# Weight halves of a float32 layer: split once and kept in DRAM, in place of split in every block

## The chip, the cores and the metric

The kernel runs on one core of a Trainium2 chip. The metric is the time of one execution on the device, in microseconds (us). TensorE (PE) multiplies; its weight loader is a row of its own in the profile (PEld). VectorE (DVE), ScalarE (ACT) and GpSimd (POOL) do the rest of the arithmetic, and SyncE (SP) and ScalarE issue the DMAs. Each engine runs its stream of instructions in order.

## The reference, cut to what matters

One layer of a hybrid model runs over 2048 prompt tokens with 16 meta tokens ahead of them, and over 8 sample sequences of 8 tokens. All is float32.

```python
h = rms_norm(x, norm_w)
proj = jnp.einsum('btd,de->bte', h, w_in)
...
new_dn_s, o_dn = run_chunks(gated_delta_chunk, dn_s, (q, k, v, g, beta), is_prompt)
...
(new_c, new_n, new_m), h_ml = run_chunks(mlstm_chunk, (ml_c, ml_n, ml_m), (q, k, v, ig, lf), is_prompt)
...
y5, new_re, new_im = s5_mixer(s5_re, s5_im, s5_u, ...)
y5 = y5 * jax.nn.sigmoid(y5 @ f32(s5_w_glu) + f32(s5_b_glu))
...
mixed = (gates[:, :, 0] * (o_dn @ w_branch_dn)
         + gates[:, :, 1] * (o_ml @ w_branch_ml)
         + gates[:, :, 2] * (o_s5 @ w_branch_s5))
x = x + mixed @ w_out
```

The products with `w_in`, `s5_w_glu`, the three `w_branch` and `w_out` are the dense products of this text. The recurrences (gated delta rule, mLSTM, S5) stand between them.

## The kernel before, in words

The tokens are columns and lie in six blocks (`BLOCKS`, L30): block 0 has the samples, the meta tokens and two tiles of 128 prompt tokens (336 columns), blocks 1 to 4 three tiles (384 columns), block 5 two (256 columns). Each block runs the whole layer: normalisation, the token rows (`rows`, "rX" and its fellows in the trace), the S5 scan, the projections, the recurrences, the mixing and the output. The order of the steps in a block is written out by hand (`PLAN0`, `PLAN`); within that a scheduler orders the instructions of each engine by priority and by its own simulated time.

A dense product (`product`, L229) multiplies in three passes, so that float32 is kept: weight and activation are each split into two exact halves, and for every 128 rows k of the weight there are three matmuls, high by high, high by low, low by high. All dense matmuls have the line 196, a helper, and write "pd". A weight tile is four such k, [128, 4, 128] float32, 256 KB, so one weight tile serves 12 matmuls. The line of the helper for two-operand arithmetic is 185.

The halves of a weight tile come from `weights` (L217): SP loads the tile "w" from DRAM (L222), ScalarE casts it to the high half "wh" (L223), and VectorE or GpSimd subtracts to get the low half "wl" (L226, L185 in the trace). In the first block every fourth subtract goes to GpSimd, later every second. This happens for every tile in every block; the weights are the same. There are four buffers for "w", three for "wh" and three for "wl" (`WB`), and the three instructions have a raised priority (`WPRIO`), so they are placed ahead of other work.

SP also issues the other loads and the transfers through DRAM: the S5 input and output ("us", "ys", stored from "s5u" and "s5y"), the S5 matrices ("s5w", "s5t") and the small blocks of the delta rule's inverse ("scrp", "scru"). ScalarE's queue issues "ox" and the output.

Of the kernel before, what the change touches and what calls it, by code (L numbers as in the profile page):

```python
# [9 lines left out]
F32 = mybir.dt.float32  # L10
F32R = mybir.dt.float32r
# [16 lines left out]
# Prompt tiles of 128 tokens per block; the first block also has the tile of samples and meta tokens.  # L28
# [8 lines left out]
WB = (4, 3, 3)  # L37
UNITS = 12
# Order of the steps of the first block and of the others: projections of q, k, v (d, m), recurrences, outputs.
# [5 lines left out]
# Buffers of temporaries: floats of a partition, and how many.  # L45
# [17 lines left out]
# Column blocks of the input projection, in the order in which the host lays them out.  # L63
CB_S5U, CB_DN, CB_ML, CB_MLO, CB_MLZ, CB_S5Z, CB_DNZ, CB_GATE = 0, 4, 16, 28, 32, 36, 40, 44

# Columns of the array of vectors.
V_NW, V_TAP, V_BG, V_DNN, V_MLN, V_S5D, V_BGLU, V_FN, V_RB, V_AL, V_LDT, V_LR, V_LI, NV = (
    0, 8, 56, 80, 81, 82, 86, 90, 98, 99, 100, 116, 132, 148)
# Columns of the array of constants.
# [34 lines left out]
class Kernel:  # L104
    def __init__(self, ctx, tc, I, O):
        self.ctx, self.tc, self.nc, self.I, self.O = ctx, tc, tc.nc, I, O
        nc = tc.nc
        self.V, self.A, self.G, self.E = nc.vector, nc.scalar, nc.gpsimd, nc.tensor
        pool = lambda n, b, **k: ctx.enter_context(tc.tile_pool(name=n, bufs=b, **k))
        self.cp = pool("const", 1)  # L110
        self.xp = pool("xn", 1)
        self.gp = pool("units", UNITS)
        self.wp = pool("weights", 2)
        self.tp = pool("temps", 2)
        self.sp = pool("small", 2)
        self.pd = pool("pdense", BANKS["pd"], space=PSUM)
        self.pr = pool("prec", 5, space=PSUM)
        self.uid = 0
        self.wn, self.rb = 0, None

# [20 lines left out]
    def temp(self, shape, tag, dt=F32):  # L141
        """A tile of a set of buffers that several steps share."""
        group = GROUP[tag]
        size, bufs = POOL[group]
        n = int(np.prod(shape[1:]))
        assert n <= size, (tag, shape)
        t = self.tp.tile([P, size], dt, name=self.name(tag), tag=group, bufs=bufs)
        v = t[:shape[0], 0:n]
        if len(shape) == 3:
            v = v.rearrange("p (a b) -> p a b", a=shape[1])  # L150
        elif len(shape) == 4:
            v = v.rearrange("p (a b c) -> p a b c", a=shape[1], b=shape[2])
        elif len(shape) == 5:
            v = v.rearrange("p (a b c d) -> p a b c d", a=shape[1], b=shape[2], c=shape[3])
        return v

    def pair(self, w, name):
        """Two tiles of the four heads, the second of width w, in one unit."""
        u = self.unit([P, 4 * P + 4 * w], name=name)
        return u[:, 0:4 * P].rearrange("p (h n) -> p h n", h=4), u[:, 4 * P:].rearrange("p (h n) -> p h n", h=4)  # L160
# [41 lines left out]
    def rsqrt(self, out, x, shape, also_sqrt=None):  # L202
        """out = 1/sqrt(x) on a small tile of positive floats: a first guess from their bits, three Newton steps."""
# [13 lines left out]
    def weights(self, src, k0):  # L217
        w = self.wp.tile([P, 4, P], F32, name=self.name("w"), tag="w", bufs=WB[0])
        h = self.wp.tile([P, 4, P], F32R, name=self.name("wh"), tag="wh", bufs=WB[1])
        l = self.wp.tile([P, 4, P], F32R, name=self.name("wl"), tag="wl", bufs=WB[2])  # L220
        with self.tc.high_priority(offset=WPRIO if self.wn > 1 else 5500):
            self.nc.sync.dma_start(w, src[:, k0:k0 + 4])  # L222
            self.A.copy(h, w)  # L223
            self.wn += 1
            pool = WPOOL if self.b else WPOOL0
            self.tt(self.G if pool and self.wn % pool == 0 else self.V, l, w, h, OP.subtract)  # L226
        return h, l
# [12 lines left out]
    def proj(self, cb):  # L240
        return self.product(self.I["wi"][cb], 8, lambda k: self.xh[k // 4][:, k % 4, :],
                            lambda k: self.xl[k // 4][:, k % 4, :], self.T)

# [1 line left out]
    def setup(self):  # L245
# [18 lines left out]
        # the row groups' bias with its sign, and the rows' factor of softplus  # L264
# [19 lines left out]
    def block(self, b):  # L284
# [20 lines left out]
        # (first column, sequences, their length): chunks over which decays are summed  # L305
        self.segs = ([(0, 8, 8), (NS, 1, NM)] if self.first else []) + [(self.p0, BLOCKS[b], P)]

    def norm(self):
        """xn^T = x^T * norm_w * rstd, as two exact halves."""
# [12 lines left out]
        if self.first:  # L322
            # x^T * norm_w in halves, for the products that need not wait for rstd
# [37 lines left out]
    def rstd_row(self, acc):  # L361
        """1/rms of every token, in every partition of a row, from squares summed over k."""
# [16 lines left out]
    def bc(self, src, c0, ns, L, p0, p1, at):  # L379
        """[p, ns, L]: of each sequence its column `at`, repeated."""  # L380
# [6 lines left out]
    def rows(self):  # L387
        T, V, A, b = self.T, self.V, self.A, self.b
        ps = self.product(self.I["ws"], 8, lambda k: self.xh[k // 4][:, k % 4, :],
# [9 lines left out]
        # softplus(u) = max(u, 0) + 2 artanh(e / (2 + e)), e = exp(-|u|)  # L399
# [17 lines left out]
        # cumulative sums by chunk: G in rows 0.., b in rows 32..  # L417
# [10 lines left out]
        # running maximum; M[:, 1 + t] is m after token t, M[:, 0] the block's first m  # L428
# [26 lines left out]
        # rows that go to all partitions: G; b - m; b + m(chunk start) - m  # L455
# [12 lines left out]
        # rows that become columns: G, G_last - G | ig - b, its state weight, -m | beta  # L468
# [11 lines left out]
    def columns(self):  # L480
        """The rows as columns of the tiles, their exponentials, and the rows as operands of products that spread them."""
# [22 lines left out]
        # halves of the rows, masked by head, as operands of the products that spread them  # L504
# [12 lines left out]
    def spread(self, i, g):  # L517
        """Rows of group g for tile i, by head, in every partition."""
# [6 lines left out]
    def dn_proj(self, n):  # L525
        """Projection, convolution and SiLU of column block n of q, k, v."""
# [35 lines left out]
    def dn_pre(self):  # L562
# [22 lines left out]
        for i, (o, n) in enumerate(self.tiles):  # L585
# [11 lines left out]
            # the squares of k are on the diagonal  # L597
# [32 lines left out]
    def dn_inv(self):  # L630
        """Inverses of the 32 x 32 blocks of I + P on the diagonal, one block per partition."""
# [22 lines left out]
    def dn_merge(self, i):  # L654
        """The whole inverse of tile i from its diagonal blocks."""
# [42 lines left out]
    def tok(self, src, o, n):  # L698
        """Token-major columns of the four heads."""
# [8 lines left out]
    def dn_tile(self, i):  # L708
# [9 lines left out]
        if n < P:  # L718
            # kept until the samples' states are updated
# [53 lines left out]
    def dn_samples_in(self, x):  # L773
        """For the samples: x -= e^G k s; returns q s, with its decay, in the upper partitions."""
# [3 lines left out]
        for h in range(4):  # L778
            # for every sequence 64 columns of k and 64 of q with those of the others zero
# [16 lines left out]
    def samples_update(self, h, states, out, left, right, decay):  # L796
        """Each sequence's state: state * decay + left^T right over its own tokens."""
# [17 lines left out]
    def factors(self, ss, other):  # L815
        """1/sqrt(ss/128 + eps*other) by token and head."""
# [8 lines left out]
    def finish(self, raw, f, gate, scale, name):  # L825
        """Branch output, feature-major and in two halves: (raw * f)^T * scale * gate(h)."""
# [16 lines left out]
    def silu2(self, cb):  # L843
        """z * (1 + tanh(z/2)) of a projected column block."""
# [92 lines left out]
    def by_sequence(self, x, tag):  # L937
        """Of the samples' columns of a head, [128, 8, 8]: for every sequence 64 columns with those of the others zero."""
# [6 lines left out]
    def ml_samples_in(self):  # L945
        """The states of the samples, and q * n."""
# [45 lines left out]
    def s5_powers(self):  # L992
        """The transition, its powers and phase, and the inputs' factor."""
# [30 lines left out]
        # powers of the transition; pw[k] = a^k  # L1024
# [10 lines left out]
        # phase of a^4  # L1035
# [4 lines left out]
        # (a - 1) / lambda  # L1040
# [13 lines left out]
    def s5_setup(self):  # L1054
        """The group matrices of four steps at a time, into DRAM: input to output, to state, from state; phases."""
# [31 lines left out]
        # powers 3, 2, 1, 0 for the inputs; 0 .. 4 for the outputs  # L1087
# [4 lines left out]
        def spread(out, pk, r, K, tag):  # L1092
            """Blocks k of out, on the diagonal of the pair: power k times r, (re + im, im - re) of r or the like."""
# [52 lines left out]
    def feat(self, d, f):  # L1146
        """Features of column block f, by step and chunk."""
        return d[:, P * f:P * f + P, 0:self.s5n].rearrange("j f c -> f j c")

    def pairs(self, d, f, j):  # L1150
        """Step j of the four pairs of groups of column block f."""
        return d[j, P * f:P * f + P, 0:self.s5n].rearrange("(a q) c -> q a c", q=32)

    def s5_scan(self, f):
# [57 lines left out]
        if self.first:  # L1212
            # samples: two chunks each from their own state
# [28 lines left out]
    def s5_finish(self):  # L1242
# [20 lines left out]
        for f in range(4):  # L1263
            ps = self.product(self.I["wg"][f], 4, lambda k: yh[:, k], lambda k: yl[:, k], T)
# [14 lines left out]
    def mix(self, j, first, last):  # L1279
        """acc += (1 + tanh(gate / 2)) * (product of branch j); the last branch leaves the sum in halves."""  # L1280
# [7 lines left out]
        for d in range(8):  # L1288
# [5 lines left out]
            pb = self.product(self.I["wb"][c], 4, lambda k: h[:, k], lambda k: l[:, k], T)  # L1294
# [9 lines left out]
    def out(self):  # L1304
# [3 lines left out]
        for d in range(8):  # L1308
            ps = self.product(self.I["wo"][d], 8, lambda k: self.mh[k // 4][:, k % 4], lambda k: self.ml_[k // 4][:, k % 4], T)
# [12 lines left out]
    def plan(self):  # L1322
        """The order in which the steps of a block are issued: where several could go on, the first goes first."""
# [191 lines left out]
```

## Time and profile before

| | us |
|---|---|
| median of 3 runs | 2884.15 |
| lowest, highest | 2884.12, 2888.75 |
| span of the profiled execution | 2881.7 |
| TensorE busy (PE) | 2695.2 |
| weight loader busy (PEld) | 2585.0 |
| VectorE busy | 2005.7 |
| GpSimd busy | 1463.6 |
| ScalarE busy | 1237.3 |

The page says on the average 140 GB/s of DMA, 404.26 MB in all. The span runs from the first to the last instruction of the profiled execution. Of that execution no time of its own is listed beside the three runs; what lies around the span is taken as the 2.45 us between it and the median. Matmuls are pipelined and their ends are modelled, so the busy time of PE is not the same as full speed; the distance between the starts of two matmuls tells the pace. A wait is put down to the engine, line and tile that came last.

### The profile page before, as it was taken

To read this page: it belongs to the slowest core of one execution; us is meant where nothing else is said; L and a number is where in the kernel's file an instruction comes from. 1 tells how busy PE (TensorE), PEld (TensorE's weight loads), DVE (VectorE), ACT (ScalarE), POOL (GpSimd) and SP (SyncE) were. 2 spreads that over 40 slices of the span, in tenths; PEclk is the share of its full clock that TensorE was granted. 3 is DMA by queue.
4 is the path that set the end of the run, shared out by engine and by line. 5 is a ranking of instruction groups with operands and counts; after the bars stand their busy time and mean duration, and the time that the engine had idled before them with its cause. 6 is when DMAs were issued, how large, how long until landed. Compare 5 with 4: busy or idle time off the path is not lost.

```text
span 2881.7 us, 49911 instructions
## 1 busy us (share of the span) xinstructions
PE 2695.2 (94%) x17416; PEld 2585.0 (90%) x17416; DVE 2005.7 (70%) x4030; ACT 1237.3 (43%) x2639; POOL 1463.6 (51%) x1545
## 2 busy tenths in 40 slices
PE   6898999998999999999998999999999999989897
PEld 5798888887999989899998989999989999978897
DVE  8789756789753488884458888345988734688854
ACT  4353334434533443443453453345335334444444
POOL 8853444355434545543464553445455345455555
PEclk9999999999999999999999999999999999998999
DMA  5544547544333455433345533345543434564544
GB/s 154 162 152 147 154 149 219 171 154 126 98 112 107 149 168 159 121 110 105 112 155 166 163 103 119 99 122 164 168 147 102 122 98 135 159 192 124 152 144 151
DMA packets 303292, 404.26 MB, mean 140 GB/s; under 512 B 109472, under 2 KB 138912, under 8 KB 303040
## 3 DMA queue, kind: packets, MB, share of 16 engines
q1 hardware_dynamic: 283248, 374.73, 43.0%
q10 hardware_dynamic: 19792, 26.34, 2.7%
q8 instruction: 137, 2.24, 0.3%
q14 instruction: 115, 0.94, 0.1%
HBM read 369.42 MB, written 31.53 MB: 139 GB/s over the span
## 4 chain that ended last, share of the span: by engine, by line
PE 40%; DVE 16%; issue 3%; DMA 3%; ACT 2%; POOL 1%; SPq 0%; DVEq 0%; ACTq 0%; POOLq 0%
PE pd L196 32%; PE pr L196 5%; DVE wl L185 2%; DVE cacc L193 2%; DVE s5a L1196 2%; PE s L196 1%; DVE invT L185 1%; DVE s5a L185 1%; DVE invU L185 1%; PE pr L200 1%; ACT wh L223 1%; DMA ox<-in_xt_dram 1%; DVE h L193 1%; POOL wl L185 1%; DVE nacc L185 1%
## 5 line engine op out<-in xcount | busy, mean ns | idle before, releaser
L185 POOL TENSOR_TENSOR wl<-w,wh 128x512 fp32r<-128x512 f32 x500 | 690.2, 1381 | 882.2 <-ACT wh L223 789.4
L196 PE MATMUL pd<-xh,wl 128*128 128x384 f32 (+2 forms) x3272 | 1083.9, 332 | 57.8 <-DVE wl L185 49.1
L223 ACT CAST wh<-w 128x512 fp32r<-128x512 f32 x1092 | 672.8, 618 | 1059.8 <-PE pd L196 742.1
L196 PE MATMUL pd<-xh,wh 128*128 128x384 f32 (+2 forms) x3272 | 1079.1, 330 | 6.5 <-ACT wh L223 5.3
L196 PE MATMUL pd<-xl,wh 128*128 128x384 f32 (+2 forms) x3272 | 1076.8, 329 | 3.5 <-DVE xl L185 3.5
L185 DVE TENSOR_TENSOR wl<-w,wh 128x512 fp32r<-128x512 f32 x592 | 469.8, 794 | 361.3 <-ACT wh L223 335.3
L196 PEld LDWEIGHTS pd<-xh,wl 128*128 128x128 f32 x3272 | 625.8, 192 | 84.0 <-DVE wl L185 63.5
L196 PEld LDWEIGHTS pd<-xh,wh 128*128 128x128 f32 x3272 | 627.9, 192 | 13.0 <-ACT wh L223 7.2
L196 PEld LDWEIGHTS pd<-xl,wh 128*128 128x128 f32 x3272 | 627.3, 192 | 9.0 <-DVE xl L185 4.7
L193 DVE SCALAR_TENSOR_TENSOR cacc<-raw,c,cacc 128x384 f32<-128x384 f32 (+2 forms) x252 | 171.0, 694 | 4.6 <-ACT cacc L182 2.5
L185 POOL TENSOR_TENSOR macc<-macc,mt 128x384 f32<-128x384 f32 (+2 forms) x96 | 106.2, 1107 | 56.8 <-DVE mt L193 54.9
L196 PE MATMUL pd<-mh,wl 128*128 128x384 f32 (+2 forms) x384 | 125.3, 329 | 5.3 <-POOL wl L185 4.2
L196 PE MATMUL pd<-mh,wh 128*128 128x384 f32 (+2 forms) x384 | 125.9, 330 | 3.6 <-DVE h L193 3.2
L196 PE MATMUL pd<-ml,wh 128*128 128x384 f32 (+2 forms) x384 | 124.4, 326 | 0.0
L193 DVE SCALAR_TENSOR_TENSOR mt<-mt,pd 128x384 f32<-128x384 f32 (+2 forms) x96 | 50.0, 521 | 96.3 <-PE pd L196 94.5
L185 POOL TENSOR_TENSOR s5a<-s5a,s5a 128x384 f32<-128x384 f32 (+2 forms) x72 | 82.6, 1156 | 66.5 <-DVE s5a L185 60.7
L185 DVE TENSOR_TENSOR invT<-invP,invU 48x31 f32<-48x31 f32 (+25 forms) x186 | 100.4, 540 | 10.4 <-DMA invP<-scrp 6.3
L1196 DVE TENSOR_TENSOR_SCAN s5a<-s5R,s5a,s5a 128x96 f32<-128x96 f32 (+2 forms) x192 | 97.5, 566 | 2.8 <-POOL s5a L185 2.7
L182 ACT ACTIVATE raw<-cacc 128x384 f32<-128x384 f32 (+2 forms) x72 | 35.9, 499 | 147.5 <-DVE cacc L193 136.5
L185 POOL TENSOR_TENSOR s5a<-s5a,s5t 128x384 f32<-128x384 f32 (+2 forms) x48 | 66.5, 1386 | 45.8 <-DVE s5a L1196 27.7
L196 PE MATMUL s<-s5U,s5w 128*128 128x96 f32 (+2 forms) x576 | 85.5, 278 | 3.4 <-DMA s5U<-us 2.3
L185 DVE TENSOR_TENSOR nacc<-nacc,nsq 128x384 f32<-128x384 f32 (+2 forms) x84 | 68.5, 816 | 28.4 <-ACT nsq L182 26.5
(396 smaller groups left out, 4744.5 us busy)
## 6 DMA issues: line engine op xcount, KB each, us to landing
w<-in_wi_dram SPq DMA_DIRECT2D x816, 256.0 KB
w<-in_wb_dram SPq DMA_DIRECT2D x144, 256.0 KB
s5w<-s5w SPq DMA_DIRECT2D x120, 256.0 KB
w<-in_wo_dram SPq DMA_DIRECT2D x96, 256.0 KB
s5t<-s5p SPq DMA_DIRECT2D x48, 192.0 KB
w<-in_wg_dram SPq DMA_DIRECT2D x24, 256.0 KB
xt<-in_xt_dram SPq DMA_DIRECT2D x32, 192.0 KB
ox<-in_xt_dram ACTq DMA_DIRECT2D x32, 192.0 KB
```

What stands on the lines that cost most here:

```text
L182: return self.A.activation(out, in_, f, **k)
L185: return eng.tensor_tensor(out, a, b, op=op)
L193: return self.V.scalar_tensor_tensor(out, a, s, b, op0=op0, op1=op1)
L196: return self.E.matmul(out, lhsT, rhs, start=start, stop=stop, **k)
L200: return self.E.transpose(out, in_, self.ident[:n, :n])
L223: self.A.copy(h, w)
L1196: V.tensor_tensor_scan(g[:, a, 1:1 + m], self.s5R[:, 4 * f + a:4 * f + a + 1].to_broadcast([P, m]), x[:, a, 0:m], g[:, a, 0:1], OP.mult, O ...
```

## The change: halves kept in DRAM

`weights` gets one buffer for both halves, `hl` [128, 2, 4, 128], with four buffers; "w" has two. Each weight tile gets a turn, 0 or 1, in the order in which tiles are first seen. In the block whose number is its turn, both halves are also stored to a DRAM tile of 512 KB of their own, and the tile is kept under its name. In every later block the kept pair is loaded with one DMA of 512 KB on SP, and neither cast nor subtract is issued. So block 0 splits all tiles and stores half of them; block 1 loads half and splits and stores the other half; blocks 2 to 5 load all. The load keeps the raised priority; the store has the normal one.

```diff
-WB = (4, 3, 3)
+WB = (2, 4)
+KEEP = 2
...
+        self.kept, self.turn = {}, {}
...
     def weights(self, src, k0):
-        w = self.wp.tile([P, 4, P], F32, name=self.name("w"), tag="w", bufs=WB[0])
-        h = self.wp.tile([P, 4, P], F32R, name=self.name("wh"), tag="wh", bufs=WB[1])
-        l = self.wp.tile([P, 4, P], F32R, name=self.name("wl"), tag="wl", bufs=WB[2])
-        with self.tc.high_priority(offset=WPRIO if self.wn > 1 else 5500):
-            self.nc.sync.dma_start(w, src[:, k0:k0 + 4])
+        name, i = src
+        g = (name, i, k0)
+        self.wn += 1
+        hl = self.wp.tile([P, 2, 4, P], F32R, name=self.name("wh"), tag="wh", bufs=WB[1])
+        with self.tc.high_priority(offset=WPRIO if self.wn > 2 else 5500):
+            if g in self.kept:
+                self.nc.sync.dma_start(hl.bitcast(F32), self.kept[g])
+                return hl[:, 0], hl[:, 1]
+            w = self.wp.tile([P, 4, P], F32, name=self.name("w"), tag="w", bufs=WB[0])
+            a = self.I[name]
+            self.nc.sync.dma_start(w, (a if i is None else a[i])[:, k0:k0 + 4])
+            h, l = hl[:, 0], hl[:, 1]
             self.A.copy(h, w)
-            self.wn += 1
             pool = WPOOL if self.b else WPOOL0
             self.tt(self.G if pool and self.wn % pool == 0 else self.V, l, w, h, OP.subtract)
+        turn = self.turn.setdefault(g, len(self.turn) % KEEP)
+        if turn == self.b:
+            d = self.tc.dram_tile([P, 2, 4, P], F32, name=self.name("wk"))
+            self.nc.sync.dma_start(d, hl.bitcast(F32))
+            self.kept[g] = d
         return h, l
```

The callers of `product` pass the name of the weight array and an index (`("wi", cb)`, `("ws", None)`, `("wg", f)`, `("wb", c)`, `("wo", d)`) where they passed the array.

## Rows read from the trace of the kernel before

**Rows 1.** The page's first line.

```profile
span 2881.7 us, 49911 instructions
```

**Rows 2.** By block (blocks 2 to 4 together): us, engines' busy us, granted clock, DMA share, GB/s.

```profile
0.00:533.00 533.00, 476.00 (x3047) 437.45 (x3048) 407.00 (x912) 220.94 (x487) 301.65 (x448) 0.96 0.52 161
533.00:1023.00 490.00, 465.98 (x2911) 450.93 (x2909) 330.54 (x636) 210.59 (x440) 242.17 (x224) 0.99 0.43 132
1023.00:2484.00 1461.00, 1400.20 (x8699) 1356.98 (x8700) 983.13 (x1890) 626.65 (x1313) 713.86 (x677) 0.98 0.44 132
2484.00:2882.00 398.00, 353.01 (x2762) 339.65 (x2761) 285.04 (x594) 179.12 (x399) 205.95 (x199) 0.94 0.51 154
```

**Rows 3.** The chain that ended last: start, us, piece; then its shares from 2600 on.

```profile
1427.52 52.62 PE pd L196 x304
...
2813.90 32.66 PE pd L196 x269
```

```profile
by line: PE pd L196 45.2%; PE pr L196 10.1%; issue 6.0%; DVE wl L185 5.9%; DVE invU L185 4.0%; DMA ox<-in_xt_dram 3.2%; DVE invT L185 2.8%; DVE h L193 1.7%; ACT wh L223 1.7%; PE pr L200 1.7%; PE s L196 1.6%; DMA s5g<-ys 1.2%; DVE rs_t L185 
```

**Rows 4.** Waits of the weight loader: us, times, longest; blocks 2 to 4, then block 5.

```profile
PEld pd L196 <- DVE wl L185: 30.9, 26, 2.6
...
PEld pr L200 <- ACT ml L182: 11.5, 3, 3.8
PEld s L196 <- POOL s5a L185: 8.7, 8, 2.0
PEld pr L200 <- DVE rX L193: 6.9, 3, 2.8
PEld s L196 <- DVE s5a L185: 6.3, 6, 1.4
PEld pd L196 <- POOL wl L185: 5.1, 3, 1.9
...
PEld pd L196 <- DVE wl L185: 17.7, 18, 2.6
PEld pd L196 <- ACT wh L223: 7.3, 8, 4.0
...
PEld pd L196 <- POOL wl L185: 2.8, 5, 1.5
```

**Rows 5.** Timeline of VectorE, then TensorE, at the start of block 2.

```profile
1064.33 1.63 DVE L185 TENSOR_TENSOR rW<-rW,rD 32x384 f32<-32x384 f32 x1
1065.99 0.55 DVE L185 TENSOR_TENSOR rC<-rC,rM 32x384 f32<-32x384 f32 x1
1066.57 0.69 DVE L185 TENSOR_TENSOR wl<-w,wh 128x512 fp32r<-128x512 f32 x1
...
1067.32 0.44 PE L196 MATMUL pd<-xh,wl 128*128 128x384 f32 x1 [1.82 <-DVE wl L185]
```

**Rows 6.** Costliest groups of the page: busy us, mean ns, idle before them, its releaser.

```profile
L185 POOL TENSOR_TENSOR wl<-w,wh 128x512 fp32r<-128x512 f32 x500 | 690.2, 1381 | 882.2 <-ACT wh L223 789.4
...
L223 ACT CAST wh<-w 128x512 fp32r<-128x512 f32 x1092 | 672.8, 618 | 1059.8 <-PE pd L196 742.1
...
L185 DVE TENSOR_TENSOR wl<-w,wh 128x512 fp32r<-128x512 f32 x592 | 469.8, 794 | 361.3 <-ACT wh L223 335.3
```

**Rows 7.** Transfers on the chain, blocks 2 and 3: start, us, piece.

```profile
1545.25 2.56 DMA out_yt_dram<-h
1550.20 2.61 DMA w<-in_wi_dram
...
1617.39 3.65 DMA w<-in_wi_dram
```

**Rows 8.** Short stretches, columns as in rows 2: dense, two with full DMA engines.

```profile
1427.00:1480.00 53.00, 53.00 (x308) 52.97 (x307) 18.55 (x27) 24.92 (x46) 30.44 (x27) 1.00 0.49 157
2030.00:2038.00 8.00, 6.69 (x38) 6.37 (x38) 7.87 (x14) 2.62 (x5) 2.09 (x2) 1.00 1.04 341
...
144.00:148.00 4.00, 4.00 (x32) 3.36 (x30) 3.61 (x6) 0.48 (x1) 3.92 (x6) 1.00 1.03 390
```

**Rows 9.** SP's queue, blocks 2 to 4: us waited, times, longest.

```profile
SPq L1173 <- DVE s5a L185: 21.0, 6, 4.2
```

More of the change, by code (lines that the diff above doesn't have):

```diff
@@ L240, in proj @@
     def proj(self, cb):
-        return self.product(self.I["wi"][cb], 8, lambda k: self.xh[k // 4][:, k % 4, :],
+        return self.product(("wi", cb), 8, lambda k: self.xh[k // 4][:, k % 4, :],
                             lambda k: self.xl[k // 4][:, k % 4, :], self.T)
@@ L388, in rows @@
         T, V, A, b = self.T, self.V, self.A, self.b
-        ps = self.product(self.I["ws"], 8, lambda k: self.xh[k // 4][:, k % 4, :],
+        ps = self.product(("ws", None), 8, lambda k: self.xh[k // 4][:, k % 4, :],
                           lambda k: self.xl[k // 4][:, k % 4, :], T)
@@ L1263, in s5_finish @@
         for f in range(4):
-            ps = self.product(self.I["wg"][f], 4, lambda k: yh[:, k], lambda k: yl[:, k], T)
+            ps = self.product(("wg", f), 4, lambda k: yh[:, k], lambda k: yl[:, k], T)
             t = self.temp([P, TMAX], "s5g")[:, :T]
@@ L1293, in mix @@
             self.act(t, pg, AF.Tanh, scale=0.5, bias=self.halfv[:, V_BG + c:V_BG + c + 1])
-            pb = self.product(self.I["wb"][c], 4, lambda k: h[:, k], lambda k: l[:, k], T)
+            pb = self.product(("wb", c), 4, lambda k: h[:, k], lambda k: l[:, k], T)
             if first:
@@ L1308, in out @@
         for d in range(8):
-            ps = self.product(self.I["wo"][d], 8, lambda k: self.mh[k // 4][:, k % 4], lambda k: self.ml_[k // 4][:, k % 4], T)
+            ps = self.product(("wo", d), 8, lambda k: self.mh[k // 4][:, k % 4], lambda k: self.ml_[k // 4][:, k % 4], T)
             x = self.temp([P, TMAX], "ox")[:, :T]
```

## The prediction, made before the changed kernel was built

> **What bounds the kernel now.** I read the span and the blocks first, then the dense stretches, then who waits for whom, and last the DMA. The profiled span is 2881.7 us [rows 1], 2.45 us below the median of the runs (2884.15); that difference I put on top of the sum. TensorE is the busiest engine in every block [rows 2]. The three blocks in the middle, with 384 columns each (three tiles of 128 tokens), take 487 us apiece; block 1 is like them, the first has 336 columns and 533 us, the last 256 columns and 398 us. By the records TensorE is idle for 57 us in the first block, 24 in block 1, 61 in the middle three and 45 in the last. That, 187 us in all, is what work off TensorE could give back at most. A dense stretch loses nothing: 304 matmuls in 52.62 us are 173 ns each, and 12 of them, one weight tile, 2.08 us; with 256 columns 269 take 32.66 us, 1.46 us a tile [rows 3]; between the two, at 336 columns, I put 1.84 us.
>
> A good part of the idle time is a wait for a weight half. The weight loader (PEld) waits for "wl" 30.9 + 5.1 = 36.0 us in the middle blocks, and for "wl" or "wh" 17.7 + 7.3 + 2.8 = 27.8 us in the last [rows 4]. Rows 5 show one such wait: TensorE stands 1.82 us for a subtract of 0.69 us, in front of which VectorE had two operations on the token rows. Streams are in order, and waits run backwards as well: the ScalarE cast stands 742 us until TensorE frees a half's buffer, and GpSimd 789 us and VectorE 335 us until that cast is done [rows 6].
>
> **Part 1, casts and subtracts leave.** A block has 1092/6 = 182 weight tiles. Blocks 2 to 5 lose all, block 1 half: 4.5 x 182 = 819 casts of 618 ns, 506 us of ScalarE, and in each of the later blocks 91 subtracts of 0.79 us on VectorE and 91 of 1.38 us on GpSimd [rows 6]. In block 1 every second tile is still split, and by the count that picks the engine these all fall to GpSimd. No engine but TensorE is the bound over a block, so this pays only through waits. Directly: the waits of rows 4 go whole, 36.0 + 27.8 us, and half of block 1's, which I take as a third of 36.0: **-70 us**.
>
> Indirectly: TensorE also waits for "ml", "s5a" and "rX", 11.5 + 8.7 + 6.9 + 6.3 = 33.4 us in the middle blocks [rows 4], and I take a third of that for the last. These come sooner when no cast or subtract stands ahead of them on ScalarE, VectorE and GpSimd, but each is a chain of its own. Of 44.5 us the ends are 0 and all; I take half, 22 us. The granted clock means 0.98 in the middle and 0.94 in the last block [rows 2], so up to 2% of 1461 us and 6% of 398 us, 53 us, go to the lower of its two levels (1.2 GHz in place of 2.4), part of it while TensorE stands anyway. A quarter back, 13 us. Together **-35 us**, bounds 0 and -98.
>
> **Part 2, the transfers double,** 512 KB for 256 KB. A load lasts 2.61 us on the chain, at worst 3.65 us [rows 7]. Full DMA engines moved 341 GB/s for 8 us, and 390 for 4 us near the start [rows 8]. The extra 0.262 MB at 341 GB/s add 0.77 us: 3.4 us a load. Four buffers, one of them in use, leave three tiles of cover, 6.2 us with 384 columns and 4.4 us with 256, so latency is covered. So is rate in the middle blocks: a dense tile asks for 0.524 MB in 2.08 us, 252 GB/s, and the rest of the traffic in that stretch is 157 less 126 for today's weights, 31 [rows 8]: 283 of 341.
>
> In the last block it is not: 0.524 MB in 1.46 us is 360 GB/s. Its other traffic is 154 GB/s x 398 us = 61.3 MB less 182 x 0.262 = 47.7 MB, 34 GB/s [rows 2]. Of 341 that leaves 307, so 1.71 us a tile, 0.25 us too slow. Dense products are 45.2% of the chain from 2600 to 2882 [rows 3]: 127 us, 87 tiles, **+22 us**. At 390 GB/s it would be 1 us; the low rate is rival (a). The Trainium skill, "DMA: Bandwidth & Descriptors", Specifications, states about 358 GB/s as the HBM limit of a core; the 390 of rows 8, short as it is, stands above it. By that page this term would be, as an estimate, 0.16 us a tile and 14 us.
>
> SP issues in order. A load will start when TensorE frees a buffer, where today it starts a subtract earlier, with the halves' buffers still in between. What else waits in SP's stream is above all the S5 store for "s5a", six times in the middle blocks, up to 4.2 us [rows 9]. The loads behind it have 6.2 - 3.4 = 2.8 us of slack with 384 columns and 4.4 - 3.4 = 1.0 us with 256, so 6 x 1.4 and, at two per block, 2 x 3.2 us show: **+15 us**, at the low end 0, if TensorE waits for the same S5 work.
>
> **Part 3, the first two blocks.** "w" has two buffers for four. A cycle of load 2.6, cast 0.62 and subtract 0.86 us (three of four on VectorE at 0.69 us, one on GpSimd [rows 5, 6]) is 4.08 us, 2.04 us a tile against 1.84. With half of block 0's 182 tiles in dense runs this is 91 x 0.20 = **+18 us**; with loads of 3.65 us 91 x 0.73 = 66 us; with no dense runs nothing. The write of a pair pins its buffer. A transfer to DRAM of 192 KB lasts 2.56 us [rows 7], so 512 KB, 0.33 MB more at 307 GB/s, 3.6 us; a buffer's cycle is then 0.62 + 0.86 + 3.6 = 5.1 us, over four buffers 1.3 us a tile: hidden behind 1.84. In block 1 one "w" cycle of 2.04 us serves two tiles: nothing. The bytes (161 GB/s now, 90 more from 91 writes of 0.524 MB in 533 us [rows 2]) fit too.
>
> **Sum.** -70 - 35 + 22 + 15 + 18 = -50 us: 2881.7 + 2.45 - 50 = **2834 us**, its own range 2805 to 2865.
>
> **The rivals.** (a) *Full DMA engines move 302 GB/s, not 341.* For it: 132 GB/s at a busy share of 0.44 is 300 at 1, 154 at 0.51 is 302 [rows 2]. Against: 341 and 390 [rows 8]. The last block then has 302 - 34 = 268 GB/s for weights, 1.96 us a tile, 0.50 us too slow, and all 182 tiles pay: 91 us for 22. With 10 us more in the middle, whose slack shrinks, 2834 + 69 + 10 = 2913 us, slower. It decides where the last block's term reaches 72 us, 0.40 us a tile: 1.85 us, 283 GB/s for weights, 317 in all. (b) *The two "w" buffers starve block 0* at 66 us, and the writes cost block 1 some 15: 2834 + 48 + 15 = 2897 us. For it: block 0 already has the most idle time and a DMA share of 0.52; against: its mean pace is 533/182 = 2.9 us a tile [rows 2]. (c) *Only the direct waits go*: the S5, "ml" and "rX" chains don't shorten: 2834 + 35 = 2869 us. (d) *Uncoupled streams give it all back*, 98 for 35: 2771 us. (e) *The change doesn't do what it says*, or its parts cancel: 2884 us. The key of a tile holds name, index and first slice, which are the same in every block, so tiles will be found; cancelling is what is left of this.
>
> **How the numbers follow.** Forecast 0.37, (a) 0.18, (b) 0.08, (c) 0.14, (d) 0.16, (e) 0.07. A measurement of this kernel can tell about 0.2%, 6 us, from no change. Faster: forecast, (c) and (d), 0.67. Same: (e), 0.07. Slower: (a) and (b), 0.26. The range from 2765 to 2918 takes in (a) and (d) and leaves what goes past them.
>
> **What would show it.** Right: no cast or subtract after block 1, no loader wait on "wl" in blocks 2 to 5, blocks 2 to 4 near 472 us, the last near 385 with DMA above 250 GB/s and some waits for the pair's load, block 0 longer by 10 to 30 us with waits behind "w". Wrong: a last block over 430 us (a); block 0 over 580 us (b); the same waits on "ml", "s5a", "rX" in the middle blocks (c), or these below 460 us (d); loads that stand long behind S5 transfers on SP.

## The result: slower by 3.2%, and the profile after

The changed kernel takes 2980.44 us (median of 4 runs, 2974.25 to 2984.43) where the kernel before takes 2886.45 us (median of 4 runs). The ratio is 1.0319, with a 95% interval of 1.0298 to 1.034. The forecast was 2834 us, with a range up to 2918.

The page of the changed kernel: first its span and busy times, then the bytes, and of the DMA issues the kept pairs.

```profile
span 2982.5 us, 47400 instructions
...
PE 2731.4 (92%) x17416; PEld 2608.2 (87%) x17416; DVE 1499.3 (50%) x3575; ACT 784.7 (26%) x1820; POOL 910.8 (31%) x1181
...
HBM read 584.12 MB, written 126.95 MB: 238 GB/s over the span
...
wh<-wk SPq DMA_DIRECT2D x819, 512.0 KB
wk<-wh SPq DMA_DIRECT2D x182, 512.0 KB
```

The change does what it says: 819 pairs are loaded, 182 stored, and ScalarE, VectorE and GpSimd lose 450 to 555 us each. It does not help. By block, cut at the first load of a block as [rows 2] are, with the same columns:

```profile
0.00:600.00 600.00, 510.20 (x3077) 456.04 (x3077) 400.62 (x917) 223.05 (x490) 296.40 (x448) 0.93 0.68 221
600.00:1112.00 512.00, 470.50 (x2881) 454.94 (x2882) 255.08 (x538) 156.74 (x345) 225.57 (x224) 0.97 0.81 264
1112.00:2564.00 1452.00, 1391.25 (x8706) 1356.38 (x8705) 667.51 (x1619) 326.54 (x769) 322.04 (x403) 0.99 0.75 232
2564.00:2983.00 419.00, 359.46 (x2757) 340.85 (x2755) 176.11 (x502) 78.36 (x216) 66.78 (x106) 0.93 0.80 262
```

Block 0 is 67 us longer than in [rows 2], block 1 22 us, the last 21 us; the three middle blocks are 9 us shorter, where some 45 were forecast (472 us each for 487). In these three VectorE works 668 us for 983, and TensorE is as idle as before (61 us). The loader's waits (us, times, longest) show what took the place of those in [rows 4]: first block 0, then blocks 2 to 4, then the last.

```profile
PEld pd L198 <- ACT wh L233: 34.5, 34, 3.2
PEld pd L198 <- DVE wh L187: 18.7, 27, 3.9
...
PEld pd L198 <- POOL wh L187: 10.6, 10, 2.9
...
PEld pr L198 <- issue: 25.0, 52, 4.6
PEld pd L198 <- DMA wh<-wk: 15.2, 11, 4.0
PEld s L198 <- POOL s5a L187: 14.7, 5, 5.8
PEld pd L198 <- DVE h L195: 10.4, 7, 2.2
...
PEld pd L198 <- DMA wh<-wk: 17.9, 25, 2.1
```

In block 0 the waits on halves are 64 us where they were 25. In the middle the 36 us on "wl" are gone; 15 us on the pairs' load have come, and the waits on "h", on "s5a" of GpSimd (8.7 before) and on "issue" (13.6 before) are longer. In block 0 the cast itself waits for its load, 216 us by these three rows of ScalarE, where it was 9:

```profile
ACT wh L233 <- DMA w<-in_wi_dram: 166.5, 89, 6.8
ACT wh L233 <- DMA w<-in_wb_dram: 36.2, 16, 4.2
ACT wh L233 <- DMA w<-in_wo_dram: 13.0, 8, 2.5
```

The chain in the last block alternates between a little matrix work and a load that is not there (start, us, piece):

```profile
2760.31 5.65 DMA wh<-wk
...
2770.83 5.51 DMA wh<-wk
...
2778.11 4.54 DMA wh<-wk
...
2788.20 5.03 DMA wh<-wk
...
2796.50 5.01 DMA wh<-wk
```

### The profile page after: what moved, and what is told of

Read it like the earlier page. It is cut to its first block, busy times and chain, and to the rows that moved or that the text cites. A ratio compares the mean times of both kernels' runs of the same rounds, so it can differ in the third digit from the quotient of the medians.

```text
span 2982.5 us, 47400 instructions
## 1 busy us (share of the span) xinstructions
PE 2731.4 (92%) x17416; PEld 2608.2 (87%) x17416; DVE 1499.3 (50%) x3575; ACT 784.7 (26%) x1820; POOL 910.8 (31%) x1181
## 4 chain that ended last, share of the span: by engine, by line
PE 54%; DMA 22%; DVE 13%; POOL 3%; issue 3%; ACT 3%; SPq 1%; ACTq 0%; DVEq 0%; POOLq 0%
PE pd L198 43%; DMA wh<-wk 7%; PE pr L198 7%; DMA w<-in_wi_dram 4%; DMA ox<-in_xt_dram 3%; PE s L198 2%; DMA wk<-wh 2%; DVE wh L187 2%; ACT wh L233 1%; DVE cacc L195 1%; DMA s5g<-ys 1%; PE pr L202 1%; DVE h L195 1%; POOL wh L187 1%; DMA w<-in_wb_dram 1%
## 5 line engine op out<-in xcount | busy, mean ns | idle before, releaser
L198 PE MATMUL pd<-xh,wh 128*128 128x384 f32 (+2 forms) x6544 | 1687.3, 334 | 79.0 <-DMA wh<-wk 41.1
L198 PEld LDWEIGHTS pd<-xh,wh 128*128 128x128 f32 x6544 | 1184.5, 194 | 115.5 <-DMA wh<-wk 40.1
L233 ACT CAST wh<-w 128x512 fp32r<-128x512 f32 x273 | 168.7, 619 | 435.4 <-DMA w<-in_wi_dram 166.5
L187 POOL TENSOR_TENSOR wh<-w,wh 128x512 fp32r<-128x512 f32 x136 | 184.9, 1359 | 305.5 <-ACT wh L233 279.5
L184 ACT ACTIVATE mt<-pd,c 128x384 f32<-128x384 f32 (+2 forms) x144 | 80.1, 556 | 364.6 <-PE pd L198 364.5
L187 DVE TENSOR_TENSOR wh<-w,wh 128x512 fp32r<-128x512 f32 x137 | 105.9, 776 | 128.1 <-ACT wh L233 127.4
L198 PEld LDWEIGHTS pd<-mh,wh 128*128 128x128 f32 x768 | 138.9, 194 | 32.3 <-DVE h L195 12.6
L198 PE MATMUL pd<-dnh,wh 128*128 128x384 f32 (+2 forms) x384 | 101.1, 327 | 8.3 <-DMA wh<-wk 4.9
L198 PE MATMUL pd<-s5h,wh 128*128 128x384 f32 (+2 forms) x384 | 102.9, 329 | 4.4 <-DMA wh<-wk 2.4
L198 PE MATMUL pd<-mlh,wh 128*128 128x384 f32 (+2 forms) x384 | 102.1, 330 | 4.0 <-ACT wh L233 3.1
```

The lines of the kernel that those rows point to most:

```text
L184: return self.A.activation(out, in_, f, **k)
L187: return eng.tensor_tensor(out, a, b, op=op)
L198: return self.E.matmul(out, lhsT, rhs, start=start, stop=stop, **k)
```

## The experiments

To compare blocks over many kernels, the table counts off a block's 182 x 12 = 2184 dense matmuls in the trace: a block lasts from its first one's start to the next block's first, block 0 from the start of the span, and the last block to the start of the last matmul of all. This cuts 6 to 10 us later than the first load does. Times are us of one profiled execution each; "whole" is the ratio to the kernel before, with its 95% interval.

Two things limit what one figure of the table can tell. In block 0 the changed kernel, e2 and e7 are one program, and it takes 608, 600 and 601 us: some 8 us in one block are not resolved. And the scheduler places the steps anew for every kernel. Compared matmul by matmul in the traces, TensorE's order is the changed kernel's in block 0 of e2 and e7 and in blocks 3 to 5 of e1; v1 and e9 share theirs in blocks 0 and 1, e8 and v1 in blocks 3 to 5. Most other pairs of rows differ in the order too, and no run takes that apart from the edit. So a small difference is not a finding, and a large one rests on the waits beside it.

| kernel | block 0 | 1 | 2 | 3 | 4 | 5 | whole |
|---|---|---|---|---|---|---|---|
| before | 541 | 490 | 487 | 487 | 486 | 383 | 1 |
| changed | 608 | 511 | 486 | 486 | 480 | 404 | 1.0319 (1.0298 to 1.034) |
| e1, 8 stores | 603 | 487 | 480 | 486 | 477 | 399 | 1.0196 (1.0164 to 1.0228) |
| e2, half of a pair loaded | 600 | 488 | 459 | 459 | 465 | 346 | 0.9814 (0.9781 to 0.9847) |
| e3, three w | 597 | 506 | 486 | 492 | 489 | 397 | 1.0279 (1.0247 to 1.0311) |
| e4, before with two w | 581 | 530 | 530 | 526 | 522 | 502 | 1.1097 (1.105 to 1.1145) |
| e5, four w, three pairs | 570 | 564 | 506 | 505 | 508 | 443 | 1.0785 (1.0759 to 1.0811) |
| e6, e5 with half kept | 573 | 505 | 500 | 495 | 504 | 396 | 1.0339 (1.03 to 1.0378) |
| e7, changed with half kept | 601 | 487 | 481 | 484 | 478 | 382 | 1.0144 (1.0127 to 1.0161) |
| e8, ring of five | 632 | 549 | 478 | 479 | 475 | 373 | 1.0402 (1.0368 to 1.0437) |
| v1, buffers swapped at block 2 | 564 | 519 | 475 | 483 | 477 | 375 | 1.0055 (1.0037 to 1.0074) |
| v2, all stores in block 0 | 618 | 469 | 484 | 479 | 480 | 383 | 1.0114 (1.0099 to 1.013) |
| e9, v1 with half of a pair loaded | 563 | 516 | 462 | 464 | 458 | 331 | 0.9715 (0.97 to 0.973) |
| e10, v1, stores on ScalarE's queue | 558 | 513 | 475 | 485 | 474 | 375 | 1.0016 (0.9998 to 1.0035) |
| e11, v1, high half's stores there | 556 | 516 | 479 | 482 | 478 | 382 | 1.0031 (1.0012 to 1.005) |
| e12, v1, stores over three blocks | 566 | 505 | 509 | 478 | 474 | 373 | 1.0136 (1.0115 to 1.0156) |

The theory after the first look had two halves: the buffers or the stores spoil blocks 0 and 1, and the doubled loads eat the gain of blocks 2 to 5. The rival to the second half was that the casts and subtracts had never held TensorE up, so that there was no gain to eat.

**e1_nostore: the stores taken out.**

```diff
-            d = self.tc.dram_tile([P, 2, 4, P], F32, name=self.name("wk"))
-            self.nc.sync.dma_start(d, hl.bitcast(F32))
-            self.kept[g] = d
+            if len(self.stored) < 8:
+                d = self.tc.dram_tile([P, 2, 4, P], F32, name=self.name("wk"))
+                self.nc.sync.dma_start(d, hl.bitcast(F32))
+                self.stored.append(d)
+            self.kept[g] = self.stored[len(self.kept) % 8]
```

> The changed kernel with 8 stores in place of 182; the later blocks load their 512 KB pairs from these 8 kept tiles in turn, so the halves are those of other weights. The loads, their number, size and order of issue stay. Theory S (the stores, by their bytes and by pinning a pair's buffer, cost block 0 its 67 us and block 1 its 21 us): block 0 falls from 608 to 560 us or less, block 1 from 511 to 490, the whole kernel to about 2910. Theory W (the two buffers of w cost block 0): block 0 stays above 590 us, the whole above 2960. Either way the last block stays at 404 us.

Measured: block 0 at 603 us, 5 less; block 1 at 487, 24 less; the last at 399; the whole at 2944 us, which fits neither theory. So by its time block 0 does not depend on the stores with these buffers, though the loader's waits on halves fall there from 64 to 39 us; e3 below shows the same kind of exchange. Block 1 does depend on them, but not on them alone: in e2, with all stores and half of each load, it is at 488 us too.

**e4_before_w2 and e3_w3: the buffers of "w" alone.**

```diff
-WB = (4, 3, 3)
+WB = (2, 3, 3)
```

> The kernel before with two buffers for w in place of four, nothing else. Theory W: every block loses, block 0 some 30 us or more, the whole kernel well over 100 us: 2990 or more, with loader waits on the cast in each block. Theory S: under 10 us in block 0, the whole within 1% of before.

Measured: 1.1097, and every block loses: 39 us in block 0, 40, 43, 39 and 36 us in blocks 1 to 4, 119 us in the last. The loader's waits over the whole of this kernel, where in the kernel before these three are about a quarter of that in all:

```profile
PEld pd L196 <- ACT wh L223: 189.4, 218, 3.4
PEld pd L196 <- DVE wl L185: 109.0, 90, 5.6
PEld pd L196 <- POOL wl L185: 93.0, 144, 3.1
```

With two buffers the cast itself is late, because its load is: in block 0 it waits for "w" 168.1 + 28.8 + 14.9 us, as long as in the changed kernel. That is theory W, at 39 of block 0's 67 us.

```diff
-WB = (2, 4)
+WB = (3, 4)
...
-    "z": (256, 4), "uc": (NTMAX * P, 2), "s5u": (TMAX, 2), "s5i": (TMAX, 2), "s5w": (512, 4),
+    "z": (256, 4), "uc": (NTMAX * P, 2), "s5u": (TMAX, 2), "s5i": (TMAX, 2), "s5w": (512, 3),
```

> The changed kernel with three buffers for w in place of two; for the room, the S5 matrices have three buffers in place of four. Theory W (a two-buffer cycle of load, cast and subtract starves block 0): block 0 falls by 30 us or more, to below 578, and its waits on the cast (34.5 us) to half. Theory S: block 0 changes by less than 15 us. Against both: the S5 scan may lose some us per block by its smaller set of buffers.

Measured: block 0 at 597 us, 11 less, which fits neither bound. The waits on halves in block 0 fall from 64 to 17 us, as theory W says. Counting the gaps between matmul starts above 0.2 us, each less 0.15, those ahead of dense matmuls fall from 123 to 70 us in block 0 and those ahead of all others rise from 46 to 84, of which 75 stand at "pr" and 9 at "s". The smaller set of S5 buffers need not be the cause: e1 has the old set, and there they go from 123 to 89 and from 46 to 71. TensorE's order differs in both. For the whole question this run is inconclusive.

**e2_halfload: the bytes of the loads halved.**

```diff
-                self.nc.sync.dma_start(hl.bitcast(F32), self.kept[g])
-                return hl[:, 0], hl[:, 1]
+                self.nc.sync.dma_start(hl[:, 0].bitcast(F32), self.kept[g][:, 0])
+                return hl[:, 0], hl[:, 0]
```

> The changed kernel, but a later block loads only the high half of a kept pair, 256 KB, and uses it in all three passes, so the low halves are left out of the products. Stores stay. Theory B (the doubled bytes of the loads ate the gain): blocks 2 to 4 fall from 486, 486 and 480 us to about 470, the last from 404 to 365, the whole kernel by some 80 to 90 us to about 2895; waits on the pair's load go nearly to nothing. Rival O (what was waited for in these blocks are chains that casts and subtracts had no part in, and the order the scheduler chose): blocks 2 to 4 stay within 5 us of 484, the last above 390.

Measured: 459, 459, 465 and 346 us, and the whole at 0.9814. Blocks 2 to 4 and the last of this kernel, columns as in [rows 2]:

```profile
1081.00:2465.00 1384.00, 1370.56 (x8704) 1343.27 (x8703) 659.16 (x1621) 327.48 (x770) 324.27 (x403) 1.00 0.46 140
2465.00:2826.00 361.00, 334.33 (x2760) 327.43 (x2758) 170.72 (x500) 77.59 (x215) 66.36 (x106) 0.97 0.56 170
```

TensorE is idle for 13 us in three blocks, where it was 61, and its granted clock is 1.00 there and 0.97 in the last block. So there is a gain: 28, 29, 21 and 37 us against the kernel before, 114 us in blocks 2 to 5, at a traffic of 140 and 170 GB/s, near that of the kernel before (132 and 154). It goes further than theory B said. The second half of each pair costs 27, 27, 14 and 57 us, 126 us. By the rows, 80 of these are idle time of TensorE (61 for 13 us and 60 for 27) and 46 are busy time (1391 for 1371 us and 359 for 334), at clocks of 0.99 for 1.00 and 0.93 for 0.97: the price is waits and, beside them, slower matmuls. The rival falls; bytes or what comes with them eat all of the gain.

**e5_w4h3 and e8_ring5: how many pairs are under way.** Bytes the same, buffers moved.

```diff
-WB = (2, 4)
+WB = (4, 3)
```

> The changed kernel with four buffers for w and three for the pairs, the same 20 KB of a partition. Theory W (two w buffers are the most of block 0's loss): block 0 returns from 608 to 560 us or less, with loader waits on the cast below 15 us. If the stores' pinning counts instead, block 0 gets worse than 608. Blocks 2 to 5 have two pairs of cover in place of three (4.2 us with 384 columns, against a load of 4.6 us): Theory L (cover, not rate, sets the later blocks) says blocks 2 to 4 above 500 us and the last above 430; if only the rate of the DMA engines counts, they stay within 5 us of 484 and 404.

Measured: with three pairs blocks 2 to 4 take 506 us each and the last 443, 22 and 39 us more than with four; block 0 comes back to 570 us, short of the 560 expected, and block 1 is 53 us longer, of which neither theory had spoken. The loader's waits on the pairs, blocks 2 to 4, then the last:

```profile
PEld pd L198 <- DMA wh<-wk: 45.7, 72, 3.7
...
PEld pd L198 <- DMA wh<-wk: 35.3, 39, 2.2
```

```diff
-WB = (2, 4)
+WB = (2, 5)
...
-            w = self.wp.tile([P, 4, P], F32, name=self.name("w"), tag="w", bufs=WB[0])
+            w = self.wp.tile([P, 2, 4, P], F32, name=self.name("w"), tag="wh", bufs=WB[1])[:, 0]
```

> The changed kernel with one ring of five 4 KB buffers for w and the pairs together, so blocks 2 to 5 have five pairs, four of cover. Theory L: the last block falls from 404 to 385 or less and blocks 2 to 4 from 484 to 475 or less, since 4 x 0.524 MB can be in flight. Theory R (the DMA engines' rate of about 300 GB/s is the bound): the last block stays within 6 us of 404, the middle ones within 5 us. Block 0 loses much in both, since two tiles and a half are all its ring holds.

Measured: with five pairs 478, 479, 475 and 373 us: 7 us less in a middle block, between the bounds of the two theories, and 31 in the last, where theory L stands. Blocks 0 and 1 are longer, 632 and 549 us. The rate shows why. A dense stretch of the last block with three pairs (e5), four (the changed kernel) and five (this run); the last two columns are DMA share and GB/s:

```profile
3000.00:3060.00 60.00, 45.32 (x341) 41.62 (x340) 5.71 (x14) 8.41 (x20) 11.74 (x16) 1.00 0.79 251
```

```profile
2880.00:2940.00 60.00, 53.00 (x411) 50.18 (x412) 9.01 (x21) 10.21 (x24) 12.51 (x17) 1.00 0.90 303
```

```profile
2900.00:2960.00 60.00, 59.05 (x483) 58.26 (x484) 10.31 (x24) 11.04 (x26) 12.51 (x17) 1.00 0.96 351
```

Three loads of 0.524 MB under way, each 5.2 us long on the chain above (the mean of the five rows is 5.15), are 3 x 0.524 / 5.2 = 302 GB/s. The 303 GB/s were not what the DMA engines can do but what three buffers ask of them. With five pairs TensorE is busy for 59.05 of the 60 us, so there it is TensorE that asks for no more than 351. The time of a load is not fixed: on the chain of the last block loads take 4.34 to 5.94 us in that stretch of e5, with two under way, and with four under way (e8) these:

```profile
2797.02 6.56 DMA wh<-wk
...
2812.60 5.81 DMA wh<-wk
...
2836.05 6.28 DMA wh<-wk
```

So a further buffer buys less than its share.

**e6_half_w4h3 and e7_half_w2h4: only every second tile kept.** In e5, and in the changed kernel:

```diff
-        if turn == self.b:
+        if turn == 0 and self.b == 0:
```

> As the run with four and three buffers, but only every second tile is kept (those stored in block 0); the other half is split in every block, by GpSimd alone by the count. 75% of the changed kernel's weight bytes in blocks 2 to 5, 91 stores in place of 182. Theory B (bytes): blocks 2 to 4 near 470 us, half of what halving all bytes gave back, the last near 375, block 0 near 555: the whole near 2845, faster than the kernel before by 1%. If three pair buffers are too few, blocks 2 to 4 stay at 485 or more.

> The same half kept, with the changed kernel's two and four buffers. Blocks 2 to 4: one w cycle of about 2.1 us serves two tiles, so they should be at 465 to 475 us and the last at 365 to 380; block 0 keeps its 608 us, block 1 falls below 500 for want of stores. The whole near 2880.

Both miss their first forecast. With three pairs the middle blocks stay at 495 to 504 us, as the last sentence of its expectation, on too few buffers, said. With four they take 481, 484 and 478 us where 465 to 475 were expected, though the last block comes to 382. A quarter of the weight bytes less is worth 3 us in a middle block, half of them 23; the casts that came back and GpSimd's subtracts take their share, and these runs don't part the two.

**v1_swap: each phase with the buffers that suit it.** Blocks 0 and 1 have the kernel before's buffers and split every tile; then that pool is closed and a ring of five pairs opened in its place.

```diff
+        if self.b >= KEEP:
+            hl = self.wp.tile([P, 2, 4, P], F32R, name=self.name("wh"), tag="wh", bufs=RING)
+            with self.tc.high_priority(offset=WPRIO):
+                self.nc.sync.dma_start(hl.bitcast(F32), self.kept[g])
+            return hl[:, 0], hl[:, 1]
...
+            self.nc.sync.dma_start(d[:, 0], h.bitcast(F32))
+            self.nc.sync.dma_start(d[:, 1], l.bitcast(F32))
...
+    def swap(self):
+        self.wctx.close()
+        self.wp = self.wctx.enter_context(self.tc.tile_pool(name="pairs", bufs=2))
```

> Blocks 0 and 1 with the kernel before's buffers (four w, three high, three low halves), all tiles split there, each pair stored once, half of them in each block, as two transfers of 256 KB; from block 2 on the same 20 KB are a ring of five pairs, loaded as in the changed kernel. If the buffers were the cause and stores cost little: block 0 at 545 to 560 us, block 1 at 490 to 500, blocks 2 to 4 near 477, the last near 373 as with the ring of five: the whole near 2860, 1% faster than before. If stores cost blocks 0 and 1 some 20 us each whatever the buffers are: 585 at most and 510, the whole near 2890, as before.

Measured: 1.0055. Block 0 is at 564 us, so buffers were 44 of its 67 us; but the stores cost 23 us there and 29 in block 1, and blocks 2 to 5 give back 12, 4, 9 and 8. That is the second case of the expectation, with block 1 beyond its 510 us. In SP's stream, blocks 0 and 1, the stores of the high half (L242) stand until the cast is done, with loads (L235) behind them:

```profile
SPq L235 <- DVE wl L189: 174.8, 120, 5.2
SPq L235 <- POOL wl L189: 110.8, 82, 6.8
SPq L242 <- ACT wh L236: 85.8, 76, 5.4
```

**v2_keep1 and e12_keep3: the stores packed or spread.** `KEEP = 1`, then `KEEP = 3`, in v1.

> As the run with the swapped buffers, but all 182 pairs are stored in block 0 and the ring of five pairs serves from block 1 on. Block 0 moves 161 + 179 = 340 GB/s at its old length, above the 300 that full DMA engines moved in the last block, so it should grow by 40 us or more, to 585 or above; block 1 near 477. If stores are hidden it is at 560 and this is the fastest of all, near 2850.

> The run with the swapped buffers, its stores spread over blocks 0 to 2 (61, 61 and 60 of them), the ring of five pairs from block 3 on. 91 stores cost 23 us in block 0 and 182 cost 77: if the price of a store grows with their density, 61 cost 10 to 13 us a block, and blocks 0 to 2 come to about 552, 502 and 500; one block less has the pairs (8 us lost): the whole near 2890. If each store costs the same, it stays at 2903 or more.

Measured: 182 stores in block 0 cost 77 us there (618 for 541); 61 in each of three blocks cost 25, 15 and 22 us, 62 in all, against 52 for 91 in each of two. A store costs 0.42 us at 182 in a block, 0.29 at 91 and 0.34 at 61: density matters at the upper end at most, and thin stores are not free. The whole of e12, 2920 us, lies beyond the 2903 of equal prices.

**e9_swap_half: v1 with half of each pair loaded,** the edit of e2.

> As the run with the swapped buffers, but from block 2 on only the high half of a pair is loaded and used in all three passes, so the low halves are left out of the products. Cover is four tiles in both. Theory B (beside cover, the bytes themselves slow the other transfers, on which the S5 chains and the output wait): blocks 2 to 4 at 460 us, the last at 345. If cover was all: blocks 2 to 4 at 473 or more, the last at 368 or more, within 5 us of the run with whole pairs.

Measured: 462, 464, 458 and 331 us. With four loads of cover in both kernels, the low halves' bytes still cost 13, 19, 19 and 44 us. Where? The loader's waits in blocks 2 to 4 of v1:

```profile
PEld pr L200 <- issue: 25.0, 49, 4.3
PEld s L200 <- POOL s5a L189: 15.9, 6, 5.1
PEld pd L200 <- DVE h L197: 7.9, 8, 2.2
PEld pr L200 <- DVE mden L183: 6.4, 4, 3.1
...
PEld pd L200 <- DMA wh<-wk: 2.1, 3, 0.9
```

and in this run:

```profile
PEld pr L200 <- issue: 13.6, 49, 1.4
PEld s L200 <- POOL s5a L189: 7.6, 6, 1.8
```

The pairs' own loads hold almost nothing up any more in these blocks (2.1 us; 5.9 in the last). Waits on "h" and "mden" are not among this run's. For "h", the output, a transfer is behind it: "h" needs "ox", and VectorE's wait for "ox" in blocks 2 to 4 is 44.8 us in v1 and 24.0 in this run, on the same loads but for their size:

```profile
DVE h L197 <- DMA ox<-in_xt_dram: 44.8, 14, 4.6
```

```profile
DVE h L197 <- DMA ox<-in_xt_dram: 24.0, 14, 3.0
```

For "s5a" no S5 transfer is seen in front of it. Its longest wait here (5.1 us), followed back in the trace, leads through VectorE's work on the token rows to ScalarE, which had stood 9.0 us behind an output transfer; the others were not followed to an end. Of the 49 us between the two kernels in these blocks, cut at the first loads, 33 are idle time of TensorE and 16 its busy time. VectorE's wait for "ox" over the whole kernel is 32.1 us before, 92.8 us in the changed kernel, 52.3 us in e2:

```profile
DVE h L195 <- DMA ox<-in_xt_dram: 92.8, 31, 5.1
```

```profile
DVE h L195 <- DMA ox<-in_xt_dram: 52.3, 29, 4.1
```

**e10_store_act and e11_high_act: the stores out of SP's stream.** In v1, both stores, then the high half's alone:

```diff
-            self.nc.sync.dma_start(d[:, 0], h.bitcast(F32))
+            self.nc.scalar.dma_start(d[:, 0], h.bitcast(F32))
```

> The run with the swapped buffers, its stores of both halves issued on ScalarE's DMA queue in place of SP's. Theory Q (SP stands at a store until its half is made, and the loads behind it come late: 85.8 us at the stores of the high half in blocks 0 and 1): block 0 falls from 564 to 550 or less, block 1 from 519 to 500 or less, the whole to 2875 or less. Theory Y (the bytes and the pinned halves of the stores): both blocks stay within 6 us. A rival to Q in its turn: ScalarE now stands at the low half's subtract, and its casts and evictions come late; then both blocks get longer than 564 and 519.

> The same with only the store of the high half on ScalarE's queue, where it stands right behind the cast that makes it and waits for nothing; the low half's store stays on SP. Theory Q: block 0 at 555 or less, block 1 at 505 or less, the whole near 2880 or below. Theory Y: within 6 us of 564 and 519.

Measured: blocks 0 and 1 at 558 and 513, and 556 and 516 us: 6 and 6, and 8 and 3 us less than v1, no more than one execution can tell; the wholes, ten runs each, are 14 and 11 us less. That is at the edge of what theory Y allows and short of theory Q, so the place in SP's stream is a small part of the stores' price, and 17 and 23 us remain in e10. The whole of e10 is at 1.0016 (0.9998 to 1.0035): no difference from the kernel before that these runs can tell. No version that computes all of it beats the kernel before.

## Why the prediction was wrong

By blocks, from the rows of the profiled executions in us, the forecast and what came:

| term | forecast | measured |
|---|---|---|
| casts and subtracts gone, blocks 2 to 5 | -99 | -114 (before to e2) |
| the pairs' bytes and SP's order, blocks 2 to 5 | +37 | +126 (e2 to changed) |
| block 0 | +18 | +67 |
| block 1 | -6 | +21 |
| sum | -50 | +100 |

**Part 1, casts and subtracts leave: right in its sum, less so in its parts.** The direct waits went as said (no loader wait on a half after block 1), and the in-order streams did hold more back: the waits on "ml", "s5a" and "rX" in the middle blocks, 33.4 us before, are 8 us in e2, where half was forecast. TensorE's idle time falls by 66 us from the kernel before to e2, where the waits were to give 86, and its busy time by 48, where the clock was to give 13. That the sum is as near as it is, is partly luck.

**Part 2, the step that failed: "3.4 us a load [...] so latency is covered".** It took a load's time from a kernel whose DMA engines were busy 44%, added the extra bytes at full rate, and found three buffers of cover enough. In the changed kernel the engines are busy 75 to 80%, and a load on the chain of the last block takes 5.2 us. Three of those are 302 GB/s at most, against 360 asked: 5.2 / 3 = 1.73 us a tile where 1.46 are wanted. The term was +22 us; e2 says 57 us in the last block. Cover is 31 of them by e8; the rest goes with the bytes even where cover is enough, as e9 shows with 44 us in v1's last block.

The figure of rival (a) came near, 303 GB/s in a dense stretch, but not its mechanism, nor its sign, a last block over 430 us (419). The engines do more when more is asked: 351 GB/s for 60 us in e8, and in the last block of the changed kernel itself 381 for 16 us, columns as before:

```profile
2596.00:2612.00 16.00, 11.28 (x80) 10.56 (x79) 14.45 (x38) 3.11 (x12) 2.58 (x4) 0.85 1.06 381
```

So 341 had been no high price for them. The Trainium skill, "DMA: Bandwidth & Descriptors", Specifications, puts the limit of HBM for a core at about 358 GB/s. The traces here go past it, by these 381 and by 364 for 60 us in block 0 of v2:

```profile
478.00:538.00 60.00, 53.67 (x286) 43.51 (x284) 29.01 (x48) 20.16 (x38) 21.62 (x18) 0.98 1.01 364
```

The Trainium skill, "HBM Reference", Latency, gives 0.2 us for an HBM access on average and 2 us under high load; 1.8 us on top of 3.4 would be 5.2, as an estimate. No run here tells that from queueing among our own loads, though their growth with the number under way (e5, e8) speaks for queueing.

In the middle blocks the term was 0 plus 8 of the 15 us of SP's order, and e2 says 68 us. Cover is a part (e8: 7 us a block, the loads' waits then nearly gone); the greater part, 13 to 19 us a block by e9, comes with the bytes at full cover, and I had not priced it at all. One piece of it is shown, the output behind "ox"; the waits on "s5a", on "mden" and on "issue" shrink with the bytes as well, and what links them to the bytes stays open, as does the share of the changed order. That the engines share their time among the transfers is what I take for the cause.

The term for SP's order, +15, was misread. The wait of [rows 9] is no store: L1173 loads "s5t", into a buffer that "s5a" has to free. In e2 SP stands there even longer (16.3 + 14.9 us in the middle blocks, for 21.0 + 3.7), and the loader waits 2.0 us for the pairs: alone it costs next to nothing.

**Part 3: buffers mis-sized, stores wrongly called hidden.** Two "w" buffers were +18 us, with 66 as the price of rival (b). They cost 39 us in block 0 of the kernel before (e4); with four of them e5 gives back 38 and v1 44 us. The load of 2.6 us was too short: at two buffers the cast stands 216 us for it. Whether the assumption "half of block 0's 182 tiles in dense runs" was too low as well, no run tells. That block 0 lost 67 us and rival (b) had said 66 is luck, since the stores, which it did not have in block 0, make up the difference. The stores, put at nothing in blocks 0 and 1, cost 23 and 29 us there with good buffers (v1), of which some 6 us a block may be SP's order (e10). In block 1 of the changed kernel leaving them out gives 24 us (e1), and halving the loads gives 23 (e2), so there it is stores and loads together. Whether the rest is their bytes or the halves they pin was not tried.

**The sum of the cases.** Rivals (a) and (b) were both priced; I gave each as an alternative to the forecast, and none for the two together. Their sum would have been 2834 + 69 + 10 + 48 + 15 = 2976 us, but by luck: worked out by block it is 599, 499, 1420 and 456 us for block 0, block 1, the middle and the last, where 600, 512, 1452 and 419 came. The middle blocks, where the cost had not been seen, are 32 us too short in it, and the last block 37 too long.

## What to carry to other kernels

When a change doubles a stream's bytes, price its loads at the time they will take under the new traffic, and check cover as loads under way x bytes / load time against the rate asked: three loads of 0.524 MB at 5.2 us gave 302 GB/s, and four, at 5.8 to 6.6 us, the 351 that were asked. Then look for the other transfers that chains wait on, as "ox" here, since they pay for the stream as well. A phase that only fills a cache keeps the buffers it had, or its own pace is the first thing lost.

## What the runs showed that had not been expected

Waits of the loader put down to "issue", in which it waits for nothing that the profile shows, move with the traffic: with "pr" they are 33.2 us before, 57.4 us in the changed kernel, 54.5 in v1 and 40.1 in e2 and e9, with single waits up to 6.0 us (v1) where the longest was 3.9. Instruction loading stands in the page's list of DMA queues (3.0 MB in the changed kernel); that this is the link was not tried.
